# One attention layer on one core: division moved into the output projection, maxima spread by transfers, and three smaller edits

## The chip, the cores and the metric

The kernel runs on one core of a Trainium2 chip. The metric is device time in microseconds (us) from the start to the end of one execution, the median of three runs. A core has five engines that each execute their own list of instructions in order and wait for one another by semaphores: TensorE (PE, with its weight loads PEld), VectorE (DVE), ScalarE (ACT), GpSimd (POOL) and SyncE (SP). SP issues nearly all transfers (DMAs) between on-chip memory and DRAM; 16 DMA engines carry them out.

## The reference

One transformer layer with two head groups that share an input projection: a convolution module (512 channels) and attention with a forget gate (8 heads of 64). Both outputs are joined, projected, gated and added to x; a gated feed-forward part follows. There are 2048 prompt frames and 8 streams of 16 new frames each, with 1024 cached frames per stream. What matters here:

```
s = einsum('bqhd,bkhd->bhqk', q, k) * HEAD_DIM ** -0.5
s = s + (cum_q[..., :, None] - cum_k[..., None, :])      # sums of log forget values
p = softmax(where(k_pos <= q_pos, s, NEG_INF), axis=-1)
attn = einsum('bhqk,bkhd->bqhd', p, v)
mix = concatenate([conv_out, attn], axis=-1) @ w_out
x = x + g1 * mix
```

All of it is in float32; the matmuls on which precision hangs are made of three products of a high and a low part.

## The kernel before

One program runs the stages one after the other, and a scheduler, working from priorities and a model of times, sorts the instructions of neighbouring pieces into one list per engine. The stages, from the start of the profiled span: modulation (to 113 us), the u and v projections (to 345), the q and k projections with their norm (to 603), attention (to about 1222), the output projection (six blocks of 360 or 368 frames, to 1433), the feed-forward part (to the end).

**Attention.** The prompt's scores are worked through in 16 steps (`STEPS`): four pairs of heads p, and in each four query blocks qb of 512. `attend` (L947 on) takes the keys of 128 frames after one another, and for each head makes a score tile s with two matmuls, L966 (key part K1 with Q1) and L967 (part K2 with Q2, which holds the remaining rows of the queries, among them the maxima), and a mask (L969). ScalarE turns s into exponentials ef (L971), and `parts_of` (L1149 on ScalarE, L1150 on VectorE or GpSimd) splits them into a high and a low part e. Three matmuls (L957) add values times e to an accumulator pv for each head; half of its 128 rows are the weighted values, the others the sum of the exponentials.

The end of a step divides: ScalarE copies sums and values apart (L988, L989), makes an approximate inverse by Ln and Exp (L991, L992), VectorE mends it with a Newton step (L993, L994) and multiplies (L995), and SP stores the result to `cat_d` (L996).

**The maxima.** The scores of a step need the largest score of each query beforehand. `score_maxima` makes the scores a first time (matmuls L927, L929; VectorE's reductions L930 into M, L934 into Z), ahead of the step. `spread_maxima` transposes Z on TensorE into pz (L941), so that the maxima of 128 queries of one head lie in one row, and VectorE writes Q2's eight rows for each head (L943): row 4h + j of 8 times a mask `bm`, which is 1 only where the row belongs to the head and to the quarter j. The eight rows of the keys' side hold -1. The first L967 of a step waits for L943.

**Loads.** `load` (L892 on) fetches a step's queries (Q1, by GpSimd's queue) and its values (vraw, L901, SP's queue), and splits the values into V. Tile vraw takes one of the three slots of tag ef, which the exponentials use as well.

**Beside attention** runs a background (`background`): the conv norm (`conv_norm`, five chunks, an inverse root by Ln, Exp and two Newton steps at L94 to L96, with its output stored to `cat_d` 1 MB at a time, L745), and the attention of the 8 streams (`sample_setup`, `sample_batch`). The latter stores a bias of 64 rows, each repeated for 16 queries, to `bias_d` (L1040) and loads a part of it as the start of each stream's score tile S (L1046), with 1 MB loads of cached keys and values (kc L1054, vc L1056). Its matmuls write the tile called lane.

**Output projection.** `project_out` goes through the six blocks. For each it loads eight chunks cr of 128 channels from `cat_d` (L1184), the four of attention first, splits them (ch, cl), and adds up 192 matmuls into eight accumulators (L1133). Then it loads x (tile xo, L1199), adds (L1141), and stores x1_d (L1203; the page calls it x_d). Tiles xo share a ring of 20 slots (tag x): 16 keep the first two blocks until their norm, which comes after the third block's sum; the third block has four left for its eight tiles.

SP's list is one queue: an instruction in it that waits holds everything behind it. Each transfer also waits for the one eight places ahead of it in SP's queue, since SP has eight semaphores for its transfers.

Of the kernel before, what the change touches and what calls it, by code (L numbers as in the profile page):

```python
# [6 lines left out]
F32 = mybir.dt.float32  # L7
# [9 lines left out]
P = 128  # L17
# [6 lines left out]
NS = 8  # L24
# [94 lines left out]
class Layer:  # L119
# [30 lines left out]
    def run(self, stop=99):  # L150
# [3 lines left out]
        with ExitStack() as ctx:  # L154
# [17 lines left out]
            self.bias_d = d.tile([NS * H, QS, PAST + QS], F32, name="bias_d")  # L172
            self.qs_d = d.tile([P, NP, P], F32, name="qs_d")
            self.open_input()
# [301 lines left out]
    def project_q_k(self):  # L476
# [45 lines left out]
        def finish(b0, b1, zs, ss, sqs, tag):  # L522
# [9 lines left out]
            newton_rsqrt(nc, y, zp.tile([P, NB], F32, tag="t", name="rt", bufs=1)[:, :n], v, 2, self.pin)  # L532
# [170 lines left out]
    def conv_norm(self, ch, sp, bank):  # L703
# [35 lines left out]
        newton_rsqrt(nc, r, sp.tile([P, 512], F32, tag="cm", name="ct")[:, :n], v, 2)  # L739
# [8 lines left out]
    def operands(self):  # L748

        nc, a = self.nc, self.a  # L750
        self.bm = self.cst.tile([P, 2, 4], F32, name="bm")
        nc.sync.dma_start(self.bm, a["bm"])
# [4 lines left out]
        for k, r, v in (("v", slice(AUX, AUX + 8), -1.0), ("t", slice(HD, HD + 2), 1.0)):  # L757
# [18 lines left out]
    def attention(self, ctx):  # L776
# [21 lines left out]
        drain(self.load(0))  # L798

        for n, (p, qb) in enumerate(STEPS):  # L800
# [3 lines left out]
            if n == 0:  # L804
                parts.append((self.last_parts(), 12))
            if n + 1 == len(STEPS):
                parts.append((self.first_weights(), 16))
# [11 lines left out]
        drain(back)  # L819
        for g in range(NP):  # L820
# [70 lines left out]
    def load(self, n):  # L891
# [8 lines left out]
        raw = self.awk.tile([P, 4, P], F32, tag="ef", name="vraw", bufs=3)  # L900
        nc.sync.dma_start(raw, self.a["o_v"][t].rearrange("(t p) e -> p t e", p=P)[:, :, p * P:(p + 1) * P])  # L901
        v = self.Vt[n % 4]
        hi, lo = (v[:, i, :, 0:3:2, :] for i in range(2))
        self.parts_of(hi, lo, raw.rearrange("p t (h e) -> p t h e", h=2), nc.vector)
        self.V.setdefault(p, []).append(v)
# [32 lines left out]
    def spread_maxima(self, Z, Q2):  # L938
# [3 lines left out]
        for h in range(2):  # L942
            nc.vector.tensor_tensor(Q2[r, h, :].rearrange("r (j q) -> r j q", j=4),  # L943
                                    pz[r, :].unsqueeze(1).broadcast_to([8, 4, P]),
                                    self.bm[r, h, :].unsqueeze(2).broadcast_to([8, 4, P]), ALU.mult)

    def attend(self, p, qb, n):  # L947
# [12 lines left out]
        for kt in range(nkt):  # L960
# [3 lines left out]
            for h in range(2):  # L964
# [6 lines left out]
                nc.scalar.activation(ef[:, off:], s[:, off:], AF.Exp)  # L971
# [13 lines left out]
        pvs, sm = (wk.tile([P, 512], F32, tag=k, name=k, bufs=1) for k in ("pvs", "sm"))  # L985
        for h in range(2):
            o, x = slice(HD * h, HD * h + HD), slice(HD - HD * h, P - HD * h)
            nc.scalar.copy(sm[o], z[h][x])  # L988
# [3 lines left out]
        self.last_exp = nc.scalar.activation(r, r, AF.Exp, scale=-1.0)  # L992
        nc.vector.tensor_tensor(sm, sm, r, ALU.mult)  # L993
        nc.vector.scalar_tensor_tensor(sm, sm, 2.0, r, ALU.subtract, ALU.mult)  # L994
        nc.vector.scalar_tensor_tensor(pvs, pvs, -1.0, sm, ALU.mult, ALU.mult)  # L995
        self.last_store = nc.sync.dma_start(self.cat_d[:, 4 + p, qb * 512:(qb + 1) * 512], pvs)  # L996

    def sample_setup(self, bank):
# [16 lines left out]
        tri = sm.tile([P, P], F32, name="tri2")  # L1015
# [24 lines left out]
        nc.sync.dma_start(self.bias_d, bias[:n].unsqueeze(1).broadcast_to([n, QS, PAST + QS]))  # L1040

    def sample_batch(self, b, bank):
# [3 lines left out]
        nc.sync.dma_start(S, self.bias_d[b * H:(b + 1) * H].rearrange("h q k -> (h q) k"))  # L1046
# [100 lines left out]
    def parts_of(self, hi, lo, raw, engine):  # L1147

        self.nc.scalar.activation(hi, raw, AF.Copy)  # L1149
        engine.tensor_tensor(lo, raw, f32(hi), ALU.subtract)  # L1150

# [503 lines left out]
```

## Time and profile before

| | us |
|---|---|
| median of three runs (lowest, highest) | 2838.67 (2837.09, 2842.48) |
| the profiled execution's own time | 2842.93 |
| its span | 2841.2 |
| TensorE busy / VectorE busy / ScalarE busy | 2729.4 / 2160.8 / 1435.3 |
| attention, 603 to 1217: length, TensorE busy | 614.0, 564.0 |
| output projection and border, 1217 to 1452: length, TensorE busy | 235.0, 220.4 |

The span runs from the first to the last instruction that the profiler recorded; the time is 1.7 us longer, and the profiled execution lies 4.3 us above the median. A row of a group gives line, engine, operation, out<-in with shapes and count, then the busy time and the mean in ns of one, and then the idle time just before them with what ended most of it. A row of the timeline gives start, duration, engine, line, and in brackets the idle time of the engine before it, with the instruction that ended it. "Clock" is the share of TensorE's full clock that was granted.

### The profile page before, as it was taken

Reading aid. Unit: us, or ns where it says so; the run is one execution under the profiler, and the core shown is the slowest. Engines: PE = TensorE matmul, PEld = TensorE weight load, DVE = VectorE, ACT = ScalarE, POOL = GpSimd, SP = SyncE. Lnnn points to the kernel's source line nnn. Section 1 sums busy time; section 2 is a strip of 40 time slices with the busy share of each in tenths; the row PEclk is TensorE's granted clock in tenths of the full one; section 3 lists DMA queues with packets and bytes.
Section 4 is the critical chain, followed back from the end, with each engine's and each line's share of the span. In section 5 each row is a group of like instructions: output and inputs, shape, how many; then the busy total and the mean of one; then the engine's idle time right before and its main releaser. Section 6 shows DMA issues by size and latency. Waiting matters only on the chain.

```text
span 2841.2 us, 48479 instructions
## 1 busy us (share of the span) xinstructions
PE 2729.4 (96%) x16536; PEld 2521.3 (89%) x16536; DVE 2160.8 (76%) x4235; ACT 1435.3 (51%) x2812; POOL 506.0 (18%) x685
## 2 busy tenths in 40 slices
PE   7899999989988999999998999999999999999999
PEld 6899988866666777788998999999999999999999
DVE  3698898988786788635488899777797778676765
ACT  4443323357675777754354455444454446555552
POOL 3454411243232222213202020000000000000000
PEclk9999999988899999999998999999999999999999
DMA  8763567674236656355667678776786669788883
GB/s 306 247 196 113 176 220 255 189 204 124 82 110 175 191 182 185 116 174 189 212 238 232 237 264 287 255 229 208 227 296 213 217 209 310 245 281 257 271 255 117
DMA packets 390024, 603.23 MB, mean 212 GB/s; under 512 B 46240, under 2 KB 249152, under 8 KB 387728
## 3 DMA queue, kind: packets, MB, share of 16 engines
q1 hardware_dynamic: 375312, 574.72, 62.6%
q0 software_dynamic: 14464, 25.42, 3.7%
q8 instruction: 130, 2.13, 0.3%
q14 instruction: 118, 0.97, 0.1%
HBM read 421.97 MB, written 178.07 MB: 211 GB/s over the span
## 4 chain that ended last, share of the span: by engine, by line
PE 78%; DMA 9%; DVE 6%; ACT 3%; issue 3%; POOL 2%; SPq 1%; DVEq 0%; ACTq 0%; POOLq 0%
PE z L1440 44%; PE z L510 7%; PE pv L957 5%; PE acc L1133 4%; PE pa L320 3%; PE pvv L340 3%; PE pg L320 3%; PE s L966 2%; PE s L967 2%; PE mx L927 2%; DMA vraw<-o_v 1%; DVE M L930 1%; DMA wraw<-w_in 1%; DMA k_d<-qp 1%; PE lane L1096 1%
## 5 line engine op out<-in xcount | busy, mean ns | idle before, releaser
L1440 PE MATMUL z<-rT,rW 128*128 128x360 f32 (+1 forms) x8316 | 1382.6, 328 | 5.1 <-ACT oR L1240 1.9
L1440 PEld LDWEIGHTS z<-rT,rW 128*128 128x128 f32 x8316 | 1379.4, 188 | 6.9 <-ACT oR L1240 2.3
L1149 ACT ACTIVATE rW<-rR 128x512 fp32r<-128x512 f32 x714 | 435.1, 617 | 397.9 <-PE z L1440 285.6
L1150 DVE TENSOR_TENSOR rW<-rR,rW 128x512 fp32r<-128x512 f32 x714 | 477.6, 673 | 154.7 <-ACT rW L1149 150.8
L698 DVE SCALAR_TENSOR_TENSOR cv<-cu,cpar,cv 128x384 f32<-128x384 f32 x580 | 311.6, 616 | 2.6 <-ACT cv L696 2.5
L957 PE MATMUL pv<-e,V 128*128 128x512 f32 (+3 forms) x960 | 265.0, 381 | 22.6 <-ACT e L1149 13.1
L957 PEld LDWEIGHTS pv<-e,V 128*128 128x128 f32 x960 | 168.9, 192 | 68.3 <-ACT e L1149 15.2
L930 DVE TENSOR_REDUCE M<-mx 128x1 f32<-128x512 f32 (+2 forms) x320 | 190.1, 605 | 50.5 <-PE mx L927 34.9
L971 ACT ACTIVATE ef<-s 128x512 f32<-128x512 f32 (+3 forms) x320 | 166.0, 529 | 104.8 <-PE s L967 46.7
L510 PE MATMUL z<-hqx,wqh 128*128 128x384 f32 (+1 forms) x768 | 196.6, 333 | 1.3 <-DVE logf L347 1.3
L1149 ACT ACTIVATE rT<-traw 128x360 fp32r<-128x360 f32 (+1 forms) x315 | 149.9, 501 | 88.8 <-DMA traw<-gt_d 52.5
L1150 POOL TENSOR_TENSOR e<-ef,e 128x512 fp32r<-128x512 f32 (+3 forms) x106 | 127.0, 1198 | 364.4 <-ACT e L1149 182.1
L1150 DVE TENSOR_TENSOR rT<-traw,rT 128x360 fp32r<-128x360 f32 (+1 forms) x315 | 158.4, 533 | 41.3 <-ACT rT L1149 41.0
L1150 DVE TENSOR_TENSOR e<-ef,e 128x512 fp32r<-128x512 f32 (+3 forms) x214 | 147.3, 698 | 40.8 <-ACT e L1149 38.1
L1149 ACT ACTIVATE e<-ef 128x512 fp32r<-128x512 f32 (+3 forms) x320 | 174.2, 565 | 4.4
L510 PEld LDWEIGHTS z<-hqx,wqh 128*128 128x128 f32 x768 | 135.7, 188 | 19.2 <-issue 15.5
L927 PE MATMUL mx<-K,Q 96*128 96x512 f32 (+2 forms) x320 | 133.6, 426 | 15.3 <-DVE M L930 13.2
L1133 PE MATMUL acc<-ch,woh 128*128 128x360 f32 (+1 forms) x384 | 128.4, 336 | 9.9 <-ACT ch L1149 5.0
L1368 DVE TENSOR_TENSOR rR<-rR 128x512 f32<-128x512 f32 (+1 forms) x136 | 90.5, 683 | 54.6 <-DMA rR<-w_down 50.0
L966 PE MATMUL s<-Q,K 128*128 128x512 f32 (+3 forms) x320 | 126.7, 397 | 3.2 <-ACT ef L971 3.0
L1133 PE MATMUL acc<-ch,wol 128*128 128x360 f32 (+1 forms) x384 | 128.1, 334 | 0.0
L510 PE MATMUL z<-hqx,wql 128*128 128x384 f32 (+1 forms) x384 | 126.4, 329 | 0.0
(306 smaller groups left out, 3955.5 us busy)
## 6 DMA issues: line engine op xcount, KB each, us to landing
rR<-sup_d SPq DMA_DIRECT2D x176, 256.0 KB
rR<-w_gate SPq DMA_DIRECT2D x132, 256.0 KB
traw<-gt_d SPq DMA_DIRECT2D x154, 180.0 KB
rR<-w_down SPq DMA_DIRECT2D x104, 256.0 KB
rR<-sdn_d SPq DMA_DIRECT2D x96, 256.0 KB
rR<-w_up SPq DMA_DIRECT2D x88, 256.0 KB
sup_d<-rR SPq DMA_DIRECT2D x88, 256.0 KB
wa<-w_ada SPq DMA_DIRECT2D x16, 1024.0 KB
```

Source lines behind the costliest of these rows:

```text
L320: nc.tensor.matmul(pz[:, :n], w[:, m], x[:, :n], start=(c == 0 and k == 0), stop=(c == CB - 1 and k == 2))
L510: nc.tensor.matmul(z[:, :n], w[:, m], x[:, :n], start=(c == 0 and k == 0), stop=(c == CB - 1 and k == 2))
L698: self.pin(nc.vector.scalar_tensor_tensor(dst, src, w, acc[i], ALU.mult, ALU.add))
L927: nc.tensor.matmul(mx[:, :w], Q2[0:AUX, h, j * P:(j + 1) * P], K2[kb][0:AUX, h, :w], start=True, stop=not diag)
L930: nc.vector.tensor_reduce(M[:, i, kb:kb + 1], mx[:, :w], AX.X, ALU.max)
L957: nc.tensor.matmul(z[h][:, off:], V[kt // 4][:, v, kt % 4, h:h + 2, :].rearrange("p b c -> p (b c)"), e[:, x, off:], start=(kt == 0 and i ...
L966: nc.tensor.matmul(s[:, off:], K1[kb][:, h, sl], Q1[:, h, off:], start=True, stop=False)
L971: nc.scalar.activation(ef[:, off:], s[:, off:], AF.Exp)
L1133: self.nc.tensor.matmul(z[:, :n], w[:, m], y, start=(first and i == 0 and k == 0), stop=(last and i == len(terms) - 1 and k == 2))
L1149: self.nc.scalar.activation(hi, raw, AF.Copy)
L1150: engine.tensor_tensor(lo, raw, f32(hi), ALU.subtract)
L1440: nc.tensor.matmul(z, W[:, x, m], t[:, y, :w], start=(k == 0 and i == 0), stop=(k == n - 1 and i == 2))
```

## The change

Five edits:

1. A step of attention stores its values undivided. ScalarE copies each head's accumulator whole (zc); SP stores the row of sums to `sum_d` and the 64 rows of values to `cat_d`. `inverses` (a step later) loads the sums as 128 partitions of 8, VectorE inverts them, and SP stores them to `inv_d`. The output projection loads, for each attention chunk, the two heads' inverses, each broadcast over 64 partitions, into a tile inv of tag x, the ring of the xo tiles, and multiplies cr by it.
2. Maxima reach Q2 by transfers: VectorE copies pz's eight rows to mrow, and eight DMAs of one row of 128 each write them, end to end, into a single row of Q2 for the two heads. The keys' side holds one row of -1 instead of eight. `bm` goes.
3. The bias of the streams is stored once per row (260 KB instead of 4160), and each S is loaded by eight transfers that repeat a row 16 times.
4. vraw has a slot of its own (tag vr), and the copy into V is issued later in the weave and ordered behind an exponential (`last_piece`).
5. The q/k norm and the conv norm make one Newton step instead of two.

```
-            newton_rsqrt(nc, y, zp.tile([P, NB], F32, tag="t", name="rt", bufs=1)[:, :n], v, 2, self.pin)
+            newton_rsqrt(nc, y, zp.tile([P, NB], F32, tag="t", name="rt", bufs=1)[:, :n], v, 1, self.pin)
...
-        raw = self.awk.tile([P, 4, P], F32, tag="ef", name="vraw", bufs=3)
+        raw = self.awk.tile([P, 4, P], F32, tag="vr", name="vraw", bufs=1)
         nc.sync.dma_start(raw, self.a["o_v"][t].rearrange("(t p) e -> p t e", p=P)[:, :, p * P:(p + 1) * P])
         v = self.Vt[n % 4]
+        self.V.setdefault(p, []).append(v)
+        yield
         hi, lo = (v[:, i, :, 0:3:2, :] for i in range(2))
-        self.parts_of(hi, lo, raw.rearrange("p t (h e) -> p t h e", h=2), nc.vector)
-        self.V.setdefault(p, []).append(v)
+        self.after(self.parts_of(hi, lo, raw.rearrange("p t (h e) -> p t h e", h=2), nc.vector), self.last_piece)
...
         nc.tensor.transpose(pz, Z, self.ident)
-        for h in range(2):
-            nc.vector.tensor_tensor(Q2[r, h, :].rearrange("r (j q) -> r j q", j=4),
-                                    pz[r, :].unsqueeze(1).broadcast_to([8, 4, P]),
-                                    self.bm[r, h, :].unsqueeze(2).broadcast_to([8, 4, P]), ALU.mult)
+        m = self.lp.tile([P, P], F32R, tag="mrow", name="mrow", bufs=1)
+        nc.vector.tensor_copy(m[r], pz[r])
+        for i in range(8):
+            nc.sync.dma_start(f32(Q2[AUX:AUX + 1, i // 4, i % 4 * P:(i % 4 + 1) * P]), f32(m[AUX + i:AUX + i + 1]))
...
-        pvs, sm = (wk.tile([P, 512], F32, tag=k, name=k, bufs=1) for k in ("pvs", "sm"))
+        zc = wk.tile([P, 2, 512], F32, tag="zc", name="zc", bufs=1)
+        t = slice(qb * 512, qb * 512 + 512)
         for h in range(2):
-            o, x = slice(HD * h, HD * h + HD), slice(HD - HD * h, P - HD * h)
-            nc.scalar.copy(sm[o], z[h][x])
-            nc.scalar.copy(pvs[o], z[h][o])
-        r = wk.tile([P, 512], F32, tag="rs", name="rs", bufs=1)
-        nc.scalar.activation(r, sm, AF.Ln)
-        self.last_exp = nc.scalar.activation(r, r, AF.Exp, scale=-1.0)
-        nc.vector.tensor_tensor(sm, sm, r, ALU.mult)
-        nc.vector.scalar_tensor_tensor(sm, sm, 2.0, r, ALU.subtract, ALU.mult)
-        nc.vector.scalar_tensor_tensor(pvs, pvs, -1.0, sm, ALU.mult, ALU.mult)
-        self.last_store = nc.sync.dma_start(self.cat_d[:, 4 + p, qb * 512:(qb + 1) * 512], pvs)
+            self.last_exp = nc.scalar.copy(zc[:, h], z[h])
+            o, x = slice(HD * h, HD * h + HD), HD - HD * h
+            nc.sync.dma_start(self.sum_d[2 * p + h:2 * p + h + 1, t], zc[x:x + 1, h])
+            self.last_store = nc.sync.dma_start(self.cat_d[o, 4 + p, t], zc[o, h])
+
+    def inverses(self, p, qb):
+
+        nc = self.nc
+        t = slice(qb * 512, qb * 512 + 512)
+        r = self.awk.tile([P, 2, 4], F32, tag="inv", name="inv")
+        nc.sync.dma_start(r, self.sum_d[2 * p:2 * p + 2, t].rearrange("h (a c) -> a h c", c=4))
+        yield
+        nc.vector.reciprocal(r, r)
+        nc.sync.dma_start(self.inv_d[2 * p:2 * p + 2, t].rearrange("h (a c) -> a h c", c=4), r)
...
-        nc.sync.dma_start(self.bias_d, bias[:n].unsqueeze(1).broadcast_to([n, QS, PAST + QS]))
+        nc.sync.dma_start(self.bias_d, bias[:n])
...
-        nc.sync.dma_start(S, self.bias_d[b * H:(b + 1) * H].rearrange("h q k -> (h q) k"))
+        for h in range(H):
+            nc.sync.dma_start(S[h * QS:(h + 1) * QS], self.bias_d[b * H + h:b * H + h + 1].broadcast_to([QS, PAST + QS]))
...
                 if c < 4:
                     nc.scalar.activation(raw, raw, AF.Silu, bias=self.cpar[:, c, CW + 2:CW + 3], scale=self.cpar[:, c, CW + 1:CW + 2])
+                else:
+                    inv = sp.tile([P, NW], F32, tag="x", name="inv", bufs=20)[:, :n]
+                    for h in range(2):
+                        load = nc.sync.dma_start(inv[HD * h:HD * h + HD], self.inv_d[2 * (c - 4) + h:2 * (c - 4) + h + 1, b0:b1].broadcast_to([HD, n]))
+                        if bi < 2:
+                            self.queued(load)
+                    nc.vector.tensor_tensor(raw, raw, inv, ALU.mult)
                 self.parts_of(hh, hl, raw, nc.vector)
```

The new lines shift the numbers by 8 to 22: L927 becomes L935, L941 becomes L949, L967 becomes L975, L1184 becomes L1199, L1199 and L1203 become L1221 and L1225.

How the lists of the engines change, at three places. First TensorE at the fourth step of attention, before; mx is a maxima tile, pz the transposition, s a score tile, and L967 the score matmul that needs the maxima:

```order
L941 MATMUL pz<-ident,Z_6636 128x128
L927 MATMUL mx<-K_6661,Q_6645 128x128
L929 MATMUL mx<-masks 128x128
L967 MATMUL s<-Q_6667,K_6643 128x512 x2
L927 MATMUL mx<-K_6661,Q_6645 128x256
```

And now, L975 being that score matmul:

```order
L949 MATMUL pz<-ident,Z_6621 128x128
L935 MATMUL mx<-K_6646,Q_6630 128x128
L937 MATMUL mx<-masks 128x128
L935 MATMUL mx<-K_6646,Q_6630 128x256
L937 MATMUL mx<-masks 128x128
L935 MATMUL mx<-K_6646,Q_6630 128x384
L937 MATMUL mx<-masks 128x128
L935 MATMUL mx<-K_6646,Q_6630 128x512
L937 MATMUL mx<-masks 128x128
L975 MATMUL s<-Q_6652,K_6628 128x512 x2
```

Two rows stood between the transposition and the score, and now eight do: three more pairs of maxima matmuls moved ahead of it.

Second, SP at the border from attention to the output projection, before; the last cat_d<-pvs is the last step's store, cr the first block's chunks, raw weights, catS the streams' output:

```order
L996 DMA cat_d<-pvs 128x512
L842 DMA raw<-w_out 128x512 x8
L1307 DMA sp_13307<-ident 128x128
L1184 DMA cr<-cat_d 128x368 x4
L1157 DMA raw<-w_out 128x512 x2
L996 DMA cat_d<-pvs 128x512
L821 DMA cat_d<-catS 128x128 x4
L1184 DMA cr<-cat_d 128x368
```

And now; the last two sum_d and cat_d rows are the last step's, and inv<-sum_d, inv_d<-inv are `inverses`:

```order
L1199 DMA cr<-cat_d 128x368
L998 DMA sum_d<-zc 1x512
L999 DMA cat_d<-zc 64x512
L828 DMA cat_d<-catS 128x128
L1006 DMA inv<-sum_d 128x2x4
L828 DMA cat_d<-catS 128x128 x3
L1009 DMA inv_d<-inv 128x2x4
L1207 DMA inv<-inv_d 64x368 x2
L1199 DMA cr<-cat_d 128x368
```

Three of the first four chunks were issued ahead of the last step's store and stand now, with their inverses, behind the whole way of the last step's sums.

Third, SP between the third and the fourth block of the output projection, before; xo<-xT loads x, x_d<-xo stores the sums, and r_d ends the third block:

```order
L1184 DMA cr<-cat_d 128x360 x2
L1203 DMA x_d<-xo 128x360 x4
L1199 DMA xo<-xT 128x360 x4
L1184 DMA cr<-cat_d 128x360
L1203 DMA x_d<-xo 128x360 x4
L1199 DMA xo<-xT 128x360 x4
L1219 DMA r_d<-ssum 128x360
```

And now:

```order
L1366 DMA traw<-ht_d 128x368 x4
L1225 DMA x_d<-xo 128x360 x4
L1221 DMA xo<-xT 128x360 x4
L1225 DMA x_d<-xo 128x360 x4
L1207 DMA inv<-inv_d 64x360 x4
L1241 DMA r_d<-ssum 128x360
L1207 DMA inv<-inv_d 64x360 x4
```

Where the fourth block's x followed the third block's last stores, its inverses follow them now, and the block's first matmul needs these.

More of the change, by code (lines that the diff above doesn't have):

```diff
@@ L171, in run @@
             self.sdn_d = d.tile([3, 4, 4, P, 512], F32, name="sdn_d")
-            self.bias_d = d.tile([NS * H, QS, PAST + QS], F32, name="bias_d")
+            self.bias_d = d.tile([NS * H, PAST + QS], F32, name="bias_d")
             self.qs_d = d.tile([P, NP, P], F32, name="qs_d")
+            self.sum_d = d.tile([H, T], F32, name="sum_d")
+            self.inv_d = d.tile([H, TT], F32, name="inv_d")
             self.open_input()
@@ L738, in conv_norm @@
         nc.scalar.activation(r, r, AF.Exp, scale=-0.5)
-        newton_rsqrt(nc, r, sp.tile([P, 512], F32, tag="cm", name="ct")[:, :n], v, 2)
+        newton_rsqrt(nc, r, sp.tile([P, 512], F32, tag="cm", name="ct")[:, :n], v, 1)
         yield
@@ L750, in operands @@
         nc, a = self.nc, self.a
-        self.bm = self.cst.tile([P, 2, 4], F32, name="bm")
-        nc.sync.dma_start(self.bm, a["bm"])
         self.Z = [self.cst.tile([P, P], F32, name=f"Z_{i}") for i in range(2)]
         aux = {}
-        for k, r, v in (("v", slice(AUX, AUX + 8), -1.0), ("t", slice(HD, HD + 2), 1.0)):
+        for k, r, v in (("v", slice(AUX, AUX + 1), -1.0), ("t", slice(HD, HD + 2), 1.0)):
             aux[k] = self.lp.tile([P, P], F32, name="aux" + k)
@@ L797, in attention @@
         self.V = {}
-        drain(self.load(0))
+        first = self.load(0)
+        next(first)
+        next(first)
+        nc.sync.dma_start(self.inv_d[:, T:], self.ones[0:H])
         for n, (p, qb) in enumerate(STEPS):
@@ L805, in attention @@
                 parts.append((self.last_parts(), 12))
+                parts.append((first, 4))
+            else:
+                parts.append((self.inverses(*STEPS[n - 1]), 2))
             if n + 1 == len(STEPS):
@@ L819, in attention @@
         drain(back)
+        drain(self.inverses(*STEPS[-1]))
         for g in range(NP):
@@ L970, in attend @@
                 ef = wk.tile([P, 512], F32, tag="ef", name="ef", bufs=3)
-                nc.scalar.activation(ef[:, off:], s[:, off:], AF.Exp)
+                self.last_piece = nc.scalar.activation(ef[:, off:], s[:, off:], AF.Exp)
                 pool, tag = self.eslots[self.ecount % len(self.eslots)]
@@ L1014, in sample_setup @@
         nc.sync.dma_start(lf, a["clfT"])
-        tri = sm.tile([P, P], F32, name="tri2")
+        tri = sm.tile([P, 4, P], F32, tag="pT", name="tri2", bufs=2)[:, 0]
         nc.sync.dma_start(tri, a["tri_s"])
@@ L1147, in parts_of @@
     def parts_of(self, hi, lo, raw, engine):
-        self.nc.scalar.activation(hi, raw, AF.Copy)
+        copy = self.nc.scalar.activation(hi, raw, AF.Copy)
         engine.tensor_tensor(lo, raw, f32(hi), ALU.subtract)
+        return copy
     def split_rows(self, hi, lo, src, ring, tag):
@@ L1616, in host_layout @@
                             for w in range(2)], 1))
-    bm = np.zeros((P, 2, 4), np.float32)
-    for h in range(2):
-        for j in range(4):
-            bm[AUX + 4 * h + j, h, j] = 1
-    r["bm"] = bm
     r["sel"] = np.concatenate([
```

1 line of the change is left out of this document (added).

## The prediction

> **What bounds the kernel now.** I read the page first, for the busy time of each engine over the whole span:
>
> ```profile
> span 2841.2 us, 48479 instructions
> PE 2729.4 (96%) x16536; PEld 2521.3 (89%) x16536; DVE 2160.8 (76%) x4235; ACT 1435.3 (51%) x2812; POOL 506.0 (18%) x685
> ```
>
> TensorE is busy 96% of the time, so anything that doesn't take time from TensorE or fill its holes is worth nothing. Where the holes are, the windows by stage tell (each row: length, busy time of PE, PEld, DVE, ACT, POOL, granted clock, DMA share, GB/s):
>
> ```profile
> 345.00:603.00 258.00, 256.39 (x1544) 216.60 (x1544) 236.32 (x579) 85.25 (x178) 62.80 (x104) 1.00 0.71 227
> 603.00:1217.00 614.00, 564.04 (x3173) 410.57 (x3171) 478.24 (x825) 432.21 (x868) 179.08 (x175) 0.94 0.50 147
> 1623.00:2841.00 1218.00, 1213.50 (x7344) 1213.20 (x7344) 934.29 (x1787) 598.30 (x1166) 20.00 (x12) 1.00 0.76 244
> ```
>
> The q/k projection and the feed-forward part leave TensorE 2 and 5 us idle. Attention (603 to 1217) leaves 50, at a clock of 0.94. Cut in three:
>
> ```profile
> 603.00:880.00 277.00, 243.85 (x1044) 169.10 (x1042) 230.55 (x391) 187.22 (x385) 88.31 (x88) 0.91 0.40 114
> 880.00:960.00 80.00, 68.42 (x391) 53.33 (x391) 52.40 (x96) 47.37 (x93) 24.09 (x25) 0.86 0.81 218
> 960.00:1217.00 257.00, 251.78 (x1740) 188.15 (x1739) 195.29 (x340) 197.62 (x390) 66.67 (x62) 1.00 0.51 162
> ```
>
> Up to 880, VectorE is busy 83% (230.55 of 277), and TensorE loses 33 us idle and about 22 to the clock (243.85 x 0.09). From 960 on TensorE is the bound. Between lies a stretch with a DMA share of 0.81 and the lowest clock. That VectorE is what TensorE waits for in front shows in the group of the maxima's matmuls (after the bar: idle time before them, and who ended it):
>
> ```profile
> L927 PE MATMUL mx<-K,Q 96*128 96x512 f32 (+2 forms) x320 | 133.6, 426 | 15.3 <-DVE M L930 13.2
> ```
>
> **Part 1: the values loaded apart, the bias stored once.** The value tile of a step came in a slot of the exponentials (tag ef), its copy ended ScalarE's idle time, and SP issued its load late:
>
> ```profile
> L1149 ACT ACTIVATE V<-vraw 128x512 fp32r<-128x512 f32 x16 | 10.1, 632 | 30.3 <-DMA vraw<-o_v 30.3
> ...
> 603.53 0.40 SPq L901 DMA_DIRECT2D vraw<-o_v  x1
> 611.44 0.63 ACT L1149 ACTIVATE V<-vraw 128x512 fp32r<-128x512 f32 x1 [4.90 <-DMA vraw<-o_v]
> 613.08 1.06 PE L519 MATMUL ssq<-sq,hsum 128*32 128x256 f32 x2 [4.82 <-ACT sq L514]
> ...
> 899.59 0.56 SPq L1040 DMA_DIRECT2D bias_d<-bias  x1
> 902.14 0.39 SPq L901 DMA_DIRECT2D vraw<-o_v  x1
> 927.17 0.63 ACT L1149 ACTIVATE V<-vraw 128x512 fp32r<-128x512 f32 x1 [12.45 <-DMA vraw<-o_v]
> 928.37 0.80 PE L957 MATMUL pv<-e,V 128*128 128x512 f32 x1 [10.36 <-ACT e L1149]
> ```
>
> Two of these waits reach TensorE: 4.82 us at 613, and 10.36 us at 928, where the value load was issued behind the bias store and landed 25 us later. After the second gap the clock is down, as one form of matmul shows before and after it:
>
> ```profile
> 904.22 0.40 PE L927 MATMUL mx<-K,Q 96*128 96x512 f32 x1
> 928.96 0.63 PE L927 MATMUL mx<-K,Q 96*128 96x512 f32 x1
> ```
>
> With a slot of its own the load stands ahead of both places, its copy (now a quarter of load's step later) behind the first exponential, and the store shrinks from 16 copies of the bias to one; the eight loads become 64, which SP issues one by one. I count 4.8 + 10.4, 3 us of cold matmuls behind each (some 13 at 0.23 more), and 5 of the other 13 us that ScalarE waited for values: **-26 us** (-15 to -30). What is late next at 928 is only the exponentials' own chain.
>
> **Part 2: VectorE's work.** These groups go or shrink:
>
> ```profile
> L993 DVE TENSOR_TENSOR sm<-sm,rs 128x512 f32<-128x512 f32 x16 | 12.3, 768 | 4.4 <-ACT rs L992 4.2
> L994 DVE SCALAR_TENSOR_TENSOR sm<-sm,rs 128x512 f32<-128x512 f32 x16 | 13.5, 841 | 0.1
> L995 DVE SCALAR_TENSOR_TENSOR pvs<-pvs,sm 128x512 f32<-128x512 f32 x16 | 10.9, 682 | 0.1
> L943 DVE TENSOR_TENSOR Q<-pz,bm 8x512 fp32r<-8x512 f32 x32 | 20.9, 692 | 2.3 <-PE pz L941 1.9
> L94 DVE SCALAR_TENSOR_TENSOR ct<-cr 128x512 f32<-128x512 f32 (+1 forms) x10 | 7.6, 757 | 0.1
> L1106 DVE COPY catS<-lane 64x64 f32<-64x64 f32 x16 | 3.5, 220 | 0.3
> ```
>
> Division: 12.3 + 13.5 + 10.9 = 36.7. Spreading the maxima: 20.9, less 16 copies of 8x128 at no more than the 0.22 of the last row (3.5). One Newton step less in the conv norm: five of ten calls on each of three lines like L94, 11.4. A similar sum leaves the q/k norm, but ahead of 603, where TensorE hides it: nothing. Added are 16 reciprocals of 128x8, also at about 0.2. Half of the division and spreading and all of the conv norm lie before 880: 18.4 + 8.7 + 11.4, in all 38 of VectorE's 230 us. If VectorE alone set the pace this would come back whole; TensorE's losses there, 33 + 22, less the 8 of part 1, leave room for it. I take 60%, since waits on ScalarE and cold clocks remain: -23. Behind 880, 27 go from an engine that seldom bounds: -5. **-28 us** together (-5 to -44). ScalarE loses 64x512 copies and a Ln/Exp pair of each step, hidden behind TensorE.
>
> **Part 3: the maxima by transfer.** Today the first scores start right on VectorE's product. From the view of line 967 (idle time until the product, and times), and the timeline of the fourth step:
>
> ```profile
>   DVE Q L943: 3.5, 10
> ...
> 739.61 1.31 DVE L943 TENSOR_TENSOR Q<-pz,bm 8x512 fp32r<-8x512 f32 x2
> 740.36 1.22 PE L967 MATMUL s<-Q,K 128*128 128x512 f32 x2
> ```
>
> Head 0 is ready 0.65 us after the product begins, head 1 after 1.31. Ten waits, in nine of the 16 steps. Instead come a copy and eight row transfers in SP's queue. The nearest rows for issue and landing:
>
> ```profile
> 1219.32 1.85 SPq L1184 DMA_DIRECT2D cr<-cat_d  x4
> ...
> 1228.65 0.38 SPq L1184 DMA_DIRECT2D cr<-cat_d  x1
> 1231.07 0.70 ACT L1188 ACTIVATE cr<-cr,cpar 128x368 f32<-128x368 f32 x1 [3.35 <-DMA cr<-cat_d]
> ```
>
> An issue is 0.46 us, a landing 2.42. Head 0: 0.2 + 4 x 0.46 + 2.4 = 4.4; head 1: 6.3. That is 3.8 and 5.0 later. The new order hides some of it: TensorE's list puts more of the next step's maxima matmuls ahead of the first score. I take 2.4 lost at each of nine steps, **+22 us** (0 if all is filled, 9 x 5.0 = 45 if nothing, more under rival A). The Trainium skill ("DMA: Bandwidth & Descriptors", Rules for kernel authors) speaks against this part: many small transfers should be made one large one, since under 64 KB they are mostly overhead; its fixed cost of about 2.0 us, stated there for the GpSimd path, would make head 0's time 4.0. The landing of 2.42 here, of 180 KB, agrees with it.
>
> **Part 4: the output projection divides.** It needs the last step's sums: store, load, reciprocal, store, loads, all in SP's order. Today:
>
> ```profile
> 1221.56 0.58 ACT L988 COPY sm<-pv 64x512 f32<-64x512 f32 x1 [0.55 <-PE pv L957]
> ...
> 1225.93 0.68 PE L1133 MATMUL acc<-ch,woh 128*128 128x368 f32 x1 [4.41 <-ACT ch L1149]
> ```
>
> The copy ends at 1222.1; the sums land at 1224.6, are read back by 1227.0, inverted by 1227.3; the first block's loads stand behind this in SP's queue and land near 1230.8; a product (0.5) and ScalarE's copy (0.5) later TensorE starts, at 1231.8: **+6** (4 to 8). Then the fourth block. Its inverses share the ring of 20 slots with x, and their loads now stand behind the third block's last x:
>
> ```profile
> 1332.55 3.25 SPq L1199 DMA_DIRECT2D xo<-xT  x4
> 1336.87 2.60 SPq L1203 DMA_DIRECT2D x_d<-xo  x4
> ...
> 1328.00:1346.00 18.00, 13.15 (x80) 12.11 (x81) 9.41 (x26) 6.79 (x14) 6.93 (x8) 1.00 0.62 196
> ```
>
> A slot is free when the store issued at 1336.9 has landed, 1339.3, and SP is through with the four at 1339.5. Two loads (0.46 each), landing 2.4, product and copy 1.0: the block's first matmul at 1343.4, where today it starts in this window's third microsecond (1330.1). Of these 13 us TensorE idles some 3 today anyway: **+10** (8 to 13, with the cold clock). The Trainium skill ("TensorE: Matmul & The Clock Gate", Part 1) says that the clock halves after an idle window of about 3.4 us and needs as much sustained work to return. By it a wait of 13 us costs another 1.7; the 0.63 for 0.40 above agrees. The other blocks load ahead: 0 to 2, taken as 0. VectorE's 24 products (13 us) lie beside matmuls.
>
> **Sum.** -26 - 28 + 22 + 6 + 10 = -16. The profiled execution took 2842.9 (span 2841.2), the median is 2838.7, 4.3 below. So 2827 for a profiled one, and **2823** for the median.
>
> **Rivals.** *A, slower: the maxima come late.* SP works in order, and the rows stand behind its other work: at the seventh and eighth step behind a 1 MB store of the conv output and the read-back of sums, at three of the last six behind 1 MB loads of cached keys or values that wait for TensorE. If little is filled (9 x 4.6 = 41) and five steps wait 3 us more for such neighbours (15), part 3 costs 56 and the sum is +18: 2857. It decides from 38 us on, 4.2 a step. For it: the value load of 902 landed 25 us late behind one large store. Against: seven steps have their maxima long before their use, and that store shrinks. The Trainium skill's rule on small transfers, named above, points to A. *B, no change: VectorE's relief buys nothing,* because ScalarE's and TensorE's own chains come next: -26 + 0 + 10 (TensorE waits for itself, so more is filled) + 16 = 0: 2839. For it: PE is busy 88% up to 880. *C, much faster:* relief in full and transfers hidden: -26 - 44 + 5 + 16 = -49: 2790. For it: VectorE's 83%, and at the fourth step eight TensorE rows now stand between the transposition and the score that needs it, where two stood.
>
> **How the numbers follow.** Forecast 0.5 (its own range 2808 to 2836), A 0.2, B 0.15, C 0.15. The range runs from 2786 to 2850: it leaves out the far half of A and a little of C. About 0.2% (5.7 us) is what a measurement of this kernel can tell from no change. Faster by more: nearly all of the forecast, C and a little of B, 0.64. Within: most of B, 0.15. Slower: A and the rest, 0.21.
>
> **What would show it.** Right: no wait of ScalarE for vraw above 2 us, VectorE busy some 190 us instead of 230 up to the eighth step's end, attention shorter by 30 to 35 us, a first output matmul some 10 us after the last value matmul instead of 4, a hole of over 10 us at the fourth block. Wrong: first scores waiting over 4 us for row transfers at most steps (A); or an attention that is no shorter with VectorE idle (B); or no hole in the output projection, which would make it 16 us faster.

## The result and the profile after

The changed kernel takes 2870.73 us (median of four runs, 2862.78 to 2875.54) against 2839.09 before: a ratio of 1.01 with a 95% interval of 1.0081 to 1.0119. It is slower by 31.6 us; 2823 was forecast, and 2850 was the range's end. The profiled execution took 2874.5 us, 31.5 more than the one before, so it can stand for the difference.

First the page of the changed kernel, span and busy times:

```profile
span 2872.7 us, 48922 instructions
PE 2743.0 (95%) x16536; PEld 2536.6 (88%) x16536; DVE 2109.1 (73%) x4178; ACT 1393.8 (49%) x2748; POOL 507.8 (18%) x685
```

VectorE lost 52 us of work and ScalarE 41.5, as the edits say. TensorE has the same 16536 matmuls and is busy 14 us longer, at a mean clock of 0.97 instead of 0.978. The windows of attention, at the same places as before, and the output projection:

```profile
603.00:880.00 277.00, 252.19 (x1058) 181.25 (x1058) 196.15 (x349) 168.73 (x355) 81.78 (x84) 0.88 0.43 107
880.00:960.00 80.00, 75.43 (x416) 60.46 (x418) 57.04 (x110) 57.99 (x120) 30.61 (x32) 0.96 0.74 189
960.00:1217.00 257.00, 239.02 (x1672) 175.93 (x1663) 165.34 (x290) 159.44 (x318) 59.00 (x55) 0.94 0.55 156
1217.00:1452.00 235.00, 198.50 (x1139) 194.22 (x1138) 100.59 (x196) 87.58 (x169) 54.57 (x53) 0.92 0.62 191
```

The first row moved the way that was forecast: VectorE 196 instead of 231 busy, and more matmuls done by 880 (1058 instead of 1044). The stretch to 960 lost most of its holes (4.6 us idle instead of 11.6). But the third row, which was full before (251.8 of 257 at a clock of 1.00), has 18 us of holes and a clock of 0.94, and the fourth has 36 us of holes where it had 15.

Behind the ninth step's start the granted clock was 0.50 in five stretches, from 931, 972, 1016, 1119 and 1170 on, of 6.8 to 10.2 us each, 37 us in all; before, none lay between 945 and 1220. Three of them follow the longest single holes (4.3, 3.6 and 3.5 us). The other two follow 3.4 us in which TensorE was 54% and 39% busy, without a hole of over 1.6.

Four places in time show where the 31.5 us come in. They are read from the timelines; the steps of attention are counted from one.

| us from the span's start | before | after | difference |
|---|---|---|---|
| first score (second matmul) of the ninth step | 945.1 | 921.1 | -24 |
| end of the last value matmul | 1221.5 | 1226.6 | +5 |
| first matmul of the output projection | 1225.9 | 1238.3 | +12 |
| end of its last matmul | 1433.2 | 1465.1 | +32 |

Attention is 24 us ahead at half way and has lost 29 by its end; the border costs 7 more, the six blocks 20. The feed-forward part takes the same in both (1410 and 1409 us).

**The border.** The changed kernel's timeline: the last sums' store, reciprocal, first product, first matmul:

```profile
1227.26 0.27 SPq L998 DMA_DIRECT2D sum_d<-zc  x1
...
1231.08 0.20 DVE L1008 RECIPROCAL inv<-inv 128x8 f32<-128x8 f32 x1 [5.06 <-DMA inv<-sum_d]
...
1231.86 1.12 SPq L1207 DMA_DIRECT2D inv<-inv_d  x2
...
1237.12 0.54 DVE L1210 TENSOR_TENSOR cr<-cr,inv 128x368 f32<-128x368 f32 x1 [5.84 <-DMA inv<-inv_d]
...
1238.26 0.67 PE L1147 MATMUL acc<-ch,woh 128*128 128x368 f32 x1 [11.64 <-ACT ch L1163]
```

The way is the one that was worked out, 11.6 us of TensorE instead of 10.3. The sums came back sooner (the reciprocal starts 3.8 us after the copy's end, where 4.9 were taken), the loads later: the second of the first two was issued at 1232.4, and its product began 4.7 us later, where 2.42 were taken. How much of this is the broadcast, one row repeated over 64 partitions, stays open. The 15 products that waited for inverses began 3.0 to 7.5 us after the issue of their second load, median 3.8; plain loads of cr that ScalarE waited for in the kernel before were used 2.3 to 4.8 us after issue, median 2.5. But at the border of run e2 (below), which has no broadcast load, plain ones took 5.3 to 5.9.

The prediction's "It needs the last step's sums" holds for SP's list and not for the data: the first block has frames 0 to 367, the last step wrote frames 1536 to 2047, and the loads were issued 0.5 us after the store of the inverses without waiting for it to land. No run tried another order.

**The fourth block.** The hole is there as well, at its place (SP's queue first, then TensorE and VectorE):

```profile
1347.87 1.95 SPq L1221 DMA_DIRECT2D xo<-xT  x4
1351.15 2.29 SPq L1225 DMA_DIRECT2D x_d<-xo  x4
1353.55 2.37 SPq L1207 DMA_DIRECT2D inv<-inv_d  x4
...
1353.24 1.36 PE L1251 MATMUL pr<-sp,ssum 128*92 128x2 f32 x8 [7.11 <-DVE xo L1155]
...
1357.31 0.53 DVE L1210 TENSOR_TENSOR cr<-cr,inv 128x360 f32<-128x360 f32 x1 [0.27 <-DMA inv<-inv_d]
...
1358.49 0.67 PE L1147 MATMUL acc<-ch,woh 128*128 128x360 f32 x1 [3.90 <-ACT ch L1163]
```

The third block's last matmul ended at 1346.1, so 12.4 us pass, 10 more than before.

**The groups.** The waits for values are gone, and two others have come (after the bar: idle time before the group, and what ended it):

```profile
L1163 ACT ACTIVATE V<-vraw 128x512 fp32r<-128x512 f32 x16 | 10.1, 630 | 0.0
L1210 DVE TENSOR_TENSOR cr<-cr,inv 128x360 f32<-128x360 f32 (+1 forms) x24 | 12.8, 535 | 47.4 <-DMA inv<-inv_d 34.6 <-DMA cr<-cat_d 9.2 <-issue 3.5
L1008 DVE RECIPROCAL inv<-inv 128x8 f32<-128x8 f32 x16 | 3.2, 200 | 25.7 <-DMA inv<-sum_d 25.6
```

VectorE stood 35 us in front of products, in all blocks and not in the fourth alone, and 26 us in front of reciprocals that waited for the sums to be read back. Five of these are the border's; the other 20 lie inside attention, in VectorE's list, with reductions of maxima and splits queued behind. The prediction priced the reciprocals at 0.2 each and said nothing of their wait.

### The profile page after: what moved, and what is told of

Same layout as the page of the kernel before. It is cut to its first block, busy times and chain, and to the rows that moved or that the text cites. A ratio compares the mean times of both kernels' runs of the same rounds, so it can differ in the third digit from the quotient of the medians.

```text
span 2872.7 us, 48922 instructions
## 1 busy us (share of the span) xinstructions
PE 2743.0 (95%) x16536; PEld 2536.6 (88%) x16536; DVE 2109.1 (73%) x4178; ACT 1393.8 (49%) x2748; POOL 507.8 (18%) x685
## 5 line engine op out<-in xcount | busy, mean ns | idle before, releaser
L938 DVE TENSOR_REDUCE M<-mx 128x1 f32<-128x512 f32 (+2 forms) x320 | 188.6, 604 | 84.3 <-PE mx L935 58.2
L1164 DVE TENSOR_TENSOR e<-ef,e 128x512 fp32r<-128x512 f32 (+3 forms) x214 | 156.5, 740 | 52.7 <-ACT e L1163 48.3
L935 PE MATMUL mx<-K,Q 96*128 96x512 f32 (+2 forms) x320 | 135.9, 442 | 18.9 <-DVE M L938 18.0
L512 PEld LDWEIGHTS z<-hqx,wqh 128*128 128x128 f32 x768 | 136.0, 188 | 15.9 <-issue 12.4
L975 PE MATMUL s<-Q,K 128*128 128x512 f32 (+3 forms) x320 | 124.6, 400 | 12.5 <-DMA Q<-mrow 12.3
L974 PE MATMUL s<-Q,K 128*128 128x512 f32 (+3 forms) x320 | 126.6, 399 | 0.3 <-ACT ef L979 0.2
```

What stands on the lines that cost most here:

```text
L512: nc.tensor.matmul(z[:, :n], w[:, m], x[:, :n], start=(c == 0 and k == 0), stop=(c == CB - 1 and k == 2))
L935: nc.tensor.matmul(mx[:, :w], Q2[0:AUX, h, j * P:(j + 1) * P], K2[kb][0:AUX, h, :w], start=True, stop=not diag)
L938: nc.vector.tensor_reduce(M[:, i, kb:kb + 1], mx[:, :w], AX.X, ALU.max)
L974: nc.tensor.matmul(s[:, off:], K1[kb][:, h, sl], Q1[:, h, off:], start=True, stop=False)
L975: nc.tensor.matmul(s[:, off:], K2[kb][:, h, sl], Q2[:, h, off:], start=False, stop=not diag)
```

## The experiments

All times are medians; each ratio is to the kernel before on the same chip in the same session, where its median lay between 2837.8 and 2841.3. A difference of under 0.15 to 0.2% (4 to 6 us) is not told from none. Differences between runs of different sessions carry the 3.5 us between those medians as well.

**The maxima's rows undone in the changed kernel** (e1). The edit, back to VectorE's product:

```
-        nc.vector.tensor_copy(m[r], pz[r])
-        for i in range(8):
-            nc.sync.dma_start(f32(Q2[AUX:AUX + 1, i // 4, ...]), f32(m[AUX + i:AUX + i + 1]))
+        for h in range(2):
+            nc.vector.tensor_tensor(Q2[r, h, :]..., pz[r, :]..., self.bm[r, h, :]..., ALU.mult)
```

> The changed kernel with one part undone: the maxima reach the queries by VectorE's product with the mask again, no row transfers. Theory 1 (the row transfers come late and cost about 59 us, while the relief of VectorE is worth its 28): 2871 - 59 = 2812. Theory 2 (the relief is worth about 5, so that the transfers cost only some 36): 2871 - 36 = 2835. If the transfers cost no more than the 22 of the prediction: 2849.

2864.1 us, ratio 1.0079 (1.006 to 1.0097): 7 us less than the changed kernel, whose interval (1.0081 to 1.0119) it overlaps. Neither 59 nor 36: both theories of late maxima fall, and so does the prediction's 22. The edit also gives VectorE 16 us of work back (products of 20.9 for copies of 4.7), so what it measures is the rows less that relief.

**The output projection without inverses** (e2):

```
-                else:
-                    inv = sp.tile([P, NW], F32, tag="x", name="inv", bufs=20)[:, :n]
-                    for h in range(2):
-                        load = nc.sync.dma_start(inv[HD * h:HD * h + HD], self.inv_d[...])
-                    ...
-                    nc.vector.tensor_tensor(raw, raw, inv, ALU.mult)
```

> The changed kernel, but the output projection neither loads the inverses nor multiplies by them (left out: the division by the sums). Both theories: the border of 11.6 us goes back to about 4.4 and the holes between blocks to those of before, so 7 + 20 = 27 us less, 2844. If the holes between the blocks have another reason than the inverses' loads (the order of SP's other transfers): no more than 7 to 15 less, 2856 to 2864.

2840.0 us, ratio 1.0003 (0.9989 to 1.0016). The whole loss is gone, 31 us, 4 more than border and blocks account for. What is left of the change is no faster than the kernel before.

**The smaller edits alone** (e3): the kernel before with edits 3, 4 and 5; rs of the old division takes the values' slot (`tag="vr"`).

> The kernel before with only the smaller edits: bias stored once, values in a slot of their own (which the division's inverse shares, for lack of memory), one Newton step. Theory 1: the stalls' 26 and a part of the relief, 8: 2805. Theory 2: the stalls' 26 and hardly any relief: 2812. If the stalls were covered by other waits: 2830 to 2839.

2843.6 us, ratio 1.0008 (0.9993 to 1.0023). Nothing, though 26 us of stall were forecast to go.

**The rows alone** (e4): the kernel before with edit 2.

> The kernel before with only the maxima by row transfers. Theory 1: 2839 + 59 = 2898. Theory 2: 2839 + 36 = 2875. By the prediction's own term: 2861.

2841.0 us, ratio 1.0003 (0.9989 to 1.0017). The rows, with the relief of VectorE that comes with them, cost nothing by themselves. At the fourth step the maxima were moved ahead by as much as their way grew: the transposition stands at 714.8 instead of 736.6, the first score at 722.7 instead of 740.4. TensorE still waited 5.4 us for rows in this run's attention.

**Loads without products** (e5):

```
                             self.queued(load)
-                    nc.vector.tensor_tensor(raw, raw, inv, ALU.mult)
```

> The changed kernel with the inverses loaded as before but the 24 products left out (left out: the division by the sums), so that nothing waits for those loads. Theory W (the wait for the inverses costs the 31 us): 2840 to 2846. Theory Q (SP's queue and the DMA engines are held up by the 48 broadcast loads and the way of the sums, whoever waits for them): 2858 to 2871.

2854.2 us, ratio 1.0051 (1.0034 to 1.0068), between the two theories. Against e2 the loads cost 14 us though no product waits for them, and the products with their waits another 16 to 17 (15 and 18 where each run is set against the kernel before of its session). The windows of the output projection, first of e5, then of e2:

```profile
1225.00:1444.00 219.00, 205.31 (x1185) 203.16 (x1186) 93.78 (x183) 81.17 (x158) 56.70 (x55) 0.96 0.65 204
```

```profile
1222.00:1430.00 208.00, 199.78 (x1181) 197.66 (x1182) 92.72 (x181) 81.22 (x157) 56.05 (x54) 0.98 0.59 192
```

The same matmuls take 11 us longer with the loads in SP's list, half of it holes (13.7 against 8.2) and half a lower clock. Two ways show in the first block: counted from its first matmul, the second chunk's plain load was issued 1.5 us later than in e2, behind broadcast loads, and it was used 6.4 us after its issue instead of 5.3. A third may be the ring of x: SP waited 2.7 us in front of loads of x until inverses had landed.

**The inverses in other slots** (e6):

```
-                    inv = sp.tile([P, NW], F32, tag="x", name="inv", bufs=20)[:, :n]
+                    inv = cp.tile([P, 512], F32, tag="w", name="inv")[:, :n]
```

> The changed kernel with the inverses in three slots of the ring of the w_out loads (idle after the first block) instead of the ring of x. If the ring of x makes the hole ahead of the fourth block: that hole shrinks from 12 us to 2 or 3, 2871 - 10 = 2861. If the hole comes from the loads' late place in SP's list or their landing time: within 3 of 2871.

2865.7 us, ratio 1.0094 (1.0073 to 1.0115). The timeline of e6 at the fourth block, whose predecessor's last matmul ended at 1340.7:

```profile
1341.82 0.41 PE L1147 MATMUL acc<-ch,woh 128*128 128x360 f32 x1 [1.08 <-DVE xo L1155]
```

The hole is gone from its place, so the ring of x did make it. But the total fell by 5 us only, which is not told from none (the intervals overlap): in this run the fourth block itself takes 41.1 us instead of 36.5, and the fifth starts 4.5 us late. The loads are late at one place or another.

**More VectorE work** (e7): the kernel before, and after the store of each step:

```
+        nc.vector.tensor_tensor(sm, sm, r, ALU.mult)
+        nc.vector.scalar_tensor_tensor(sm, sm, 2.0, r, ALU.subtract, ALU.mult)
+        nc.vector.scalar_tensor_tensor(sm, sm, -1.0, r, ALU.mult, ALU.mult)
```

> The kernel before with three more VectorE operations of 128x512 at each step's end (the division's own, again, on a tile nobody reads; 37 us in all). Theory V (VectorE sets attention's pace up to 880, so its relief should have paid): half of 37 lies there, +12 to +20, 2851 to 2859. Theory P (VectorE has slack everywhere, a relief pays nothing): at most +5, 2844.

2869.6 us, ratio 1.0103 (1.0084 to 1.0123): 29 us for 37 us of work, more than theory V had. Attention ends 22 us later: 10 have come by the ninth step, and 12 come behind it, where the prediction had VectorE as an engine that seldom bounds.

**The values' slot alone** (e8): the kernel before with edit 4.

> The kernel before with only the values in a slot of their own (shared with the division's inverse for lack of memory). If the two stalls at 613 and 928 are worth what their holes are: 2839 less 15 to 26, 2813 to 2824. If the time comes back at later steps, as with the three edits together: 2836 to 2844.

2849.9 us, ratio 1.0042 (1.0028 to 1.0056). The gap of 10.36 us is gone, and the kernel is 10 us slower. Another gap, of 5.65 us, stands at the same place: TensorE waits for VectorE, and VectorE for the streams' bias, whose large store is still there. The sharing with the old division's inverse may have a part in it; e11 tries the slot without that.

**No inverses' work at all** (e9), e2 and also:

```
-            else:
-                parts.append((self.inverses(*STEPS[n - 1]), 2))
...
-        drain(self.inverses(*STEPS[-1]))
```

> The changed kernel without any of the inverses' work: no read-back of the sums, no reciprocal, no store of inverses, no broadcast loads, no products (left out: the division). The row transfers and the other edits stay. Theory H (the read-back, which waits in SP's and VectorE's lists for the sums to land, holds up the row transfers of the next step; the last four steps took 151 us with both, 139 to 142 with one of them): 10 below the 2840 of the run without loads and products, 2830. Theory N (the two don't meet): 2840.

2829.5 us, ratio 0.9972 (0.9959 to 0.9985): 10.5 below e2; set against the kernel before of its session it is 8.3 faster where e2 was 1.3, so that the read-back costs 7 to 10, as theory H had it. The windows from the ninth step to the last value matmul, of e2 and of e9 (whose profiled execution is the fastest of its ten, 6.7 under the median, so that the 19 us between them are too many):

```profile
913.00:1219.00 306.00, 278.01 (x1892) 206.24 (x1890) 192.22 (x345) 192.88 (x393) 71.28 (x69) 0.94 0.56 155
```

```profile
916.00:1203.00 287.00, 270.25 (x1900) 205.96 (x1898) 183.82 (x337) 192.08 (x393) 71.43 (x69) 0.96 0.58 170
```

One such meeting in the changed kernel, at the twelfth step:

```profile
1013.04 0.73 SPq L998 DMA_DIRECT2D sum_d<-zc  x2
...
1017.77 0.39 SPq L1006 DMA_DIRECT2D inv<-sum_d  x1
...
1018.02 0.42 PE L949 MATMUL pz<-ident,Z 128*128 128x128 f32 x1
...
1019.68 0.20 DVE L1008 RECIPROCAL inv<-inv 128x8 f32<-128x8 f32 x1 [2.35 <-DMA inv<-sum_d]
...
1020.47 0.30 DVE L951 CAST mrow<-pz 8x128 fp32r<-8x128 f32 x1
...
1020.79 5.00 SPq L953 DMA_DIRECT2D Q<-mrow  x8
...
1027.19 0.64 PE L975 MATMUL s<-Q,K 128*128 128x512 f32 x2
...
1027.62 0.60 ACT L979 ACTIVATE ef<-s 128x512 f32<-128x512 f32 x1 [5.51 <-PE s L975]
```

The maxima are transposed at 1018.4, but VectorE stands in front of the reciprocal until 1019.7 and copies them at 1020.5; SP then needs 5 us for eight rows, and the first score comes 9.2 us after the transposition began, where before it came after 1.2. ScalarE is idle for 5.5 us of that. The reciprocal's part is at most 2 us: e9, without it, takes 7.5 at this step. It is also the only step at which the copy stands behind a reciprocal; at nine of the 15 in attention a reduction of maxima (L938) does. What TensorE waited for in attention (us in all, times, longest), in the changed kernel and then in e9, shows the meeting better:

```profile
PE mx L935 <- DVE M L938: 18.0, 24, 2.5
PE s L975 <- DMA Q<-mrow: 12.3, 6, 3.6
```

```profile
PE s L972 <- DMA Q<-mrow: 12.3, 7, 3.4
PE mx L932 <- DVE M L935: 9.9, 16, 2.9
```

The wait for reductions is 18 us with rows and read-back (17.9 in e2), 9.9 without the read-back (e9) and 10.9 without the rows (e1). So it is the two together that make the reductions late. The last four steps say nearly the same: 151 us in the changed kernel, e2, e5 and e6, and 147 in e11, which have both; 139 to 142 in e1, e4, e9 and e15, which have one; but 138 in the kernel before and 146 in e3, which have neither.

The wait for the rows themselves is there without the read-back too. Its longest is at the eleventh step:

```profile
962.95 9.73 SPq L953 DMA_DIRECT2D Q<-mrow  x8
...
972.64 1.19 PE L975 MATMUL s<-Q,K 128*128 128x512 f32 x2 [3.59 <-DMA Q<-mrow]
```

SP waited for 4.6 of these 9.7 us until 1 MB loads of cached values had landed. At the fifteenth step its eight issues took 6.9 us, and TensorE waited 3.46.

**Rows for the first eight steps only** (e10): the kernel before with, in `spread_maxima`, `if n < 8:` the copy and the eight transfers, and the product otherwise.

> The kernel before with row transfers for the first eight steps and VectorE's masked product for the last eight. Theory S (the rows gain where VectorE sets the pace and the DMA engines are half idle, 12 us in the first eight steps, and lose as much in the last eight, among 1 MB loads): 2840 - 10 = 2830. If the gain in front is always given back behind: 2840.

2849.6 us, ratio 1.004 (1.0024 to 1.0055). Theory S falls, and so does the other: rows in eight steps cost 12 us here, where rows in all sixteen cost none (e4).

**The values back in the exponentials' slots** (e11), in the changed kernel:

```
-        raw = self.awk.tile([P, 4, P], F32, tag="vr", name="vraw", bufs=1)
+        raw = self.awk.tile([P, 4, P], F32, tag="ef", name="vraw", bufs=3)
```

with the split straight behind the load, as before.

> The changed kernel with the values back in a slot of the exponentials (tag ef), nothing else undone. If the own slot is worth the two stalls: 2871 + 15 to 26, 2886 to 2897. If it costs, as alone in the kernel before (+10): 2861. If it is worth nothing: within 5 of 2870.

2877.6 us, ratio 1.0142 (1.0123 to 1.016): the slot is worth 7 us here, where it cost 10 in the kernel before.

**Rows in front, bias, Newton step** (e12): e10 with edits 3 and 5.

> The kernel before with three parts: row transfers for the first eight steps only, bias stored once, one Newton step; values and division as before. If the pieces add (rows in front -10, bias and Newton step -6 as the difference of the runs with and without them): 2824. If attention gives gains back: 2836 to 2844.

2817.3 us, ratio 0.9928 (0.9913 to 0.9943): faster than both kernels, by more than the pieces. Its windows of attention:

```profile
603.00:880.00 277.00, 257.87 (x1098) 182.22 (x1098) 221.88 (x383) 189.74 (x390) 88.27 (x88) 0.91 0.40 113
880.00:960.00 80.00, 74.30 (x438) 56.85 (x437) 54.52 (x104) 53.57 (x105) 23.02 (x24) 0.91 0.80 218
960.00:1199.00 239.00, 231.41 (x1628) 173.64 (x1627) 178.30 (x310) 183.29 (x369) 63.38 (x59) 1.00 0.49 154
```

It keeps in the third row what the changed kernel lost there: a clock of 1.00.

**One Newton step alone** (e13), edit 5 in the kernel before.

> The kernel before with one Newton step instead of two in both norms, nothing else. VectorE loses 11 us of attention's first part. If a relief of VectorE pays as its load costs (29 for 37): -9, 2830. If it pays nothing: 2839.

2834.1 us, ratio 0.9979 (0.9967 to 0.9992): 5 us.

**The bias stored once, alone** (e14), edit 3 in the kernel before.

> The kernel before with the bias stored once and loaded by 64 transfers, nothing else. The 4 MB store no longer stands ahead of the values at 902. If the stall at 928 (10 us and the cold clock behind it) came from that store: 2839 - 13 = 2826. If it comes from the 1 MB loads in any case or is given back: 2836 to 2842.

2841.2 us, ratio 1.0001 (0.9986 to 1.0016). No wait of TensorE above 3 us is left in this run's attention, neither the 4.82 nor the 10.36, and the time is the same.

**Rows in all steps, bias, Newton step** (e15): e4 with edits 3 and 5.

> The kernel before with row transfers for all 16 steps, bias stored once, one Newton step; the run with rows for eight steps only took 2817. If rows hurt in the last eight steps: 2825 to 2835. If they are as good there: 2812 to 2820.

2829.9 us, ratio 0.9952 (0.9936 to 0.9968): 9 to 11 below the rows alone and 11 to 13 above e12.

**Less VectorE work in the division** (e16), in the kernel before:

```
-        nc.vector.tensor_tensor(sm, sm, r, ALU.mult)
-        nc.vector.scalar_tensor_tensor(sm, sm, 2.0, r, ALU.subtract, ALU.mult)
-        nc.vector.scalar_tensor_tensor(pvs, pvs, -1.0, sm, ALU.mult, ALU.mult)
+        nc.vector.scalar_tensor_tensor(pvs, pvs, 1.0, r, ALU.mult, ALU.mult)
```

> The kernel before without the division's Newton step: two of its three VectorE operations go, 26 us in 32 operations (left out: the exact inverse, Ln and Exp's own remains). If a relief pays as the load of three more operations cost (29 for 37): 2839 - 20 = 2819. If a relief pays nothing: 2839.

2840.5 us, ratio 1.0 (0.9986 to 1.0014). Nothing for 26 us. The second stall is in it as before, some 13 us earlier:

```profile
913.83 0.63 ACT L1147 ACTIVATE V<-vraw 128x512 fp32r<-128x512 f32 x1 [11.66 <-DMA vraw<-o_v]
...
914.99 0.80 PE L966 MATMUL s<-Q,K 128*128 128x512 f32 x1 [10.31 <-ACT ef L971]
```

## Why the prediction was wrong, step by step

The forecast was -16, from -54 for attention's relief and stalls, +22 for the rows and +16 for the output side; measured are +32. Run e2 divides the 48 us between them: without the inverses in the output projection the change is worth about nothing, where parts 1 to 3 had -32 in sum, and the inverses there cost 31, where part 4 had 16. So the larger miss is the relief that did not come.

**Part 1, "-26 us", and part 2, "-28 us", gave nothing that adds up.** The holes went as forecast: no ScalarE wait for vraw, VectorE's share down, the ninth step 24 us earlier. But stall by stall and edit by edit the total stayed: bias once 0 (e14), own slot +10 in the kernel before and -7 in the changed one (e8, e11), one Newton step -5 (e13), two division operations less 0 (e16), all three small edits 0 (e3). The step of the argument that failed is "if VectorE alone set the pace this would come back whole ... I take 60%", and in part 1 the counting of a stall at its full length. More work for VectorE does cost: 37 us more took 29 (e7). Less work gave 5 for 11 (e13) and nothing for 26 (e16). Moving the whole division out of attention, read as e1 against e3, ends attention 8.6 us earlier (1213.0 against 1221.6), for 37 us of VectorE work and 39 of ScalarE's.

Where the time goes instead is seen but not settled. In the kernel before, the second half of attention ran at a clock of 1.00 with hardly a hole. In the changed kernel, in e3 and in e4 the first half is 18 to 24 us shorter and the second 14 to 29 longer, with single holes of 2 to 4 us, several at the steps' starts, and a clock of 0.94 to 0.97. In the changed kernel the 29 us are 17 of holes and 12 of matmuls that take longer, in the stretches of a clock of 0.50. Each edit makes the scheduler write a new order, and the same edit has another worth in another order: bias and Newton step together are worth 32 us on e10 (e12), 9 to 11 on e4 (e15), and 6 to 7 on the values' slot (e3 against e8); rows are worth 0 in all steps (e4) and cost 12 in half of them (e10). A price for one edit of some 10 us is within what the order alone seems to move; no run here held the order fixed, so that is a reading of the spread, not a proof.

**Part 4, "+6" and "+10", "the other blocks load ahead: 0 to 2, taken as 0", failed in its size and left out two terms.** Taking the division's new work off the changed kernel piece by piece gives a ladder: 2870.7; without the products 2854.2 (e5); without the loads too 2840.0 (e2); without the read-back and reciprocals 2829.5 (e9). So the products with their waits cost some 17, the 48 loads some 14 by their presence, and the read-back in attention 7 to 10: about 40 us, where 16 stood. The two places named were right, and at about their price: 7.2 at the border for 6, 10 at the fourth block for 10. Missed were three things. First, the other blocks, with holes of 4.4 and 3.2 us ahead of the third and the fifth: there TensorE waits for VectorE's sum (L1155), which in the fifth stands behind products that wait for inverses. Second, the loads as work for SP and its queue, which delays what stands behind them; how much of their 14 us is SP's list, slower landing or the ring of x was not tried apart. Third, the read-back in attention: the prediction gave the reciprocals their 0.2 us each and no wait. With the rows it holds up the reductions of maxima; how much of the 7 to 10 is VectorE's wait and how much SP's list was not tried apart either.

**Part 3, "+22", was too dear.** With the relief of VectorE that belongs to them the rows cost nothing alone (e4), and in the changed kernel some 7, which is not told from none (e1). The landing was right: at the steps where the score follows closely it came 5 to 10 us after the transposition began instead of 1 to 4. But the transposition itself moved ahead. The prediction saw this in the order (eight rows instead of two) and still charged 2.4 a step. TensorE's direct wait for rows is 12.3 us in the changed kernel and 5.4 in e4. The Trainium skill ("DMA: Bandwidth & Descriptors", Rules for kernel authors) calls transfers under 64 KB mostly overhead. Here 128 of 0.5 KB left the total as it was (2841.0 against 2841.3, e4).

**The rivals.** A came near in its number (2857), and that is luck. Its mechanism is there only in part: row transfers late behind 1 MB loads at the eleventh and the fifteenth step, with holes of 3.6 and 3.5 us, out of 12.3 in all where A had 56; and the output side, which it took at 16, cost 31. B's "relief buys nothing" was right, and its sign came, an attention no shorter with VectorE less busy; its sum failed on part 4. C did not happen in this change; e12 shows that attention can be 23 us shorter (1198.6 against 1221.5).

## What to carry to other kernels

When work moves from the end of one stage into the start of the next, count what the move adds to the queues between them: here 48 loads cost 14 us with no product waiting for them. An operation that waits for a transfer stops everything behind it in its engine's list, so a read-back with reciprocals of 0.2 us each cost 7 to 10 us, more than its own length. And a hole in a profile is worth its length only if the work behind it was waiting for nothing else: put the smallest edit that closes it on the chip alone before adding its length to a sum.

## What the runs showed of the hardware

A one-row transfer of 512 bytes takes SP longer to issue than a load of 128 rows: eight of them took 5.00 us, 0.63 each from one to the next, against 0.46 for the loads of 128x368 in the kernel before. A load that repeats one DRAM row over 64 partitions took 0.44 to 0.61 us to issue, and its user, where it waited, began 3.0 to 7.5 us after that issue (median 3.8), against 2.3 to 4.8 (median 2.5) for the loads of 128 partitions in the kernel before. Stretches of a granted clock of 0.50 last 3.4, 6.8, 10.2, 13.7 or 17.1 us in attention and the output projection of the two traces, multiples of 3.4. Two of them, of 6.8 and 10.2, came behind 3.4 us in which TensorE was still 39% and 54% busy and no single hole was over 1.6 us long: many short holes did it as well as one of 3.5.
